# RMSNorm and matmul on one core: weights on the other queue, and PE transposes that carry two bf16 features as one word

## The chip, the cores and the metric

The kernel runs on one core of one Trainium2 chip. The metric is the device time of one execution in microseconds; the figure compared is the median of several runs. The names used: PE is the matmul engine (PEld its weight loads), DVE the vector engine, ACT the scalar engine, POOL the GpSimd engine, and SP the engine that here only issues DMAs. PSUM is the memory that PE writes its results to.

## The reference

`x` is 16 x 1024 rows of 512 features, `weight` is 512 x 768, all float32.

```python
rms = np.sqrt(np.mean(x ** 2, axis=-1, keepdims=True) + eps)
x_norm = x / rms * gamma
return np.matmul(x_norm, weight).astype(np.float32)
```

The kernel computes the same in another order: `gamma` is multiplied into the rows of `weight` once, the matmul runs on raw `x` cast to bf16, and the division by the rms is a scale of the result rows.

## The kernel before

The 16384 rows are cut into 32 groups of 512 (each partition holds 4 consecutive rows), and each group into two pairs: pair `j` is two tiles `t` of 128 rows. The features are cut into K = 4 slices of 128. For a pair, the work passes through the engines like this:

- SP loads a group of `x` (1 MB, line 63), into one of 8 buffers, six groups ahead of its use.
- POOL casts the pair to bf16, `xb` (line 71).
- ACT squares and sums the rows (line 77) and takes the root (line 80); DVE forms the reciprocal, `rstd` (line 82).
- PE transposes the pair's 2 x 4 blocks of 128 x 128 (line 90) into a PSUM tile `tp`, of which there are two; DVE copies `tp` to `xT` (line 92).
- PE multiplies (line 106): for each tile and each k, one matmul of 512 columns and one of 256, with `xT` as the stationary operand and the scaled weights `w_bf` as the moving one, accumulating over k in one of three PSUM buffers `ops`. Each matmul has its own weight load.
- The result is scaled by `rstd` into `ot`: the first tile by ACT (line 110), the second by DVE (line 112). There are four `ot` buffers of one group each.
- SP stores a finished group (1.5 MB, line 116).

Each engine works through its own instructions in the order in which the program writes them. In the loop over pairs this order is: load of group j/2 + 6, cast of pair j+2, squares of j+1, all eight transposes and the copy of j+1, then the matmuls of j, then (every second pair) the store. SP therefore issues the load of a group behind the store of an earlier one, and that store waits until ACT and DVE have written the group.

Ahead of the loop SP queues the first loads of `x`. ACT issues, on its own queue, the load of `gamma` (as 4 rows of 128) and four loads of weight slices. PE transposes `gamma` to `g_sb`, behind the transposes of pair 0, so that partition p holds the factor of feature k x 128 + p. DVE then scales the four weight slices into `w_bf` (line 148) as they come.

Of the kernel before, what the change touches and what calls it, by code (L numbers as in the profile page):

```python
# [12 lines left out]
F32 = mybir.dt.float32  # L13
BF16 = mybir.dt.bfloat16
# [3 lines left out]
@with_exitstack  # L18
def kernel(
    ctx: ExitStack,  # L20
    tc: tile.TileContext,
    x: bass.AP,
    gamma: bass.AP,
    weight: bass.AP,
    eps: float,
    out: bass.AP,
):
    nc = tc.nc
    P = 128

    x = x.flatten_outer_dims()
    out = out.flatten_outer_dims()
    N, D = x.shape
    _, O = out.shape
    K = D // P
    G = 4
    NG = N // (P * G)
    NP = 2 * NG
    PF = 6
    SPLITS = [(0, 512), (512, O)]  # L40


    xg = x.rearrange("(g p t) d -> g p t d", p=P, t=G)
    og = out.rearrange("(g p t) o -> g p t o", p=P, t=G)

    singles = ctx.enter_context(tc.tile_pool(name="singles", bufs=1))
    xin = ctx.enter_context(tc.tile_pool(name="xin", bufs=PF + 2))
    xbp = ctx.enter_context(tc.tile_pool(name="xb", bufs=3))
    junk = ctx.enter_context(tc.tile_pool(name="junk", bufs=2))
    stats = ctx.enter_context(tc.tile_pool(name="stats", bufs=4))  # L50
    xt_pool = ctx.enter_context(tc.tile_pool(name="xt", bufs=3))
    tpsum = ctx.enter_context(tc.tile_pool(name="tpsum", bufs=2, space=bass.MemoryType.PSUM))
    opsum = ctx.enter_context(tc.tile_pool(name="opsum", bufs=3, space=bass.MemoryType.PSUM))
    outp = ctx.enter_context(tc.tile_pool(name="out", bufs=4))

    x_tiles, xb_tiles, rstd_tiles, xT_tiles, o_tiles = {}, {}, {}, {}, {}

    def load(g, parts=1):
        xt = xin.tile([P, G, D], F32, name="xt")
        x_tiles[g] = xt  # L60
        n = G // parts
        for i in range(parts):
            nc.sync.dma_start(out=xt[:, i * n:(i + 1) * n, :], in_=xg[g, :, i * n:(i + 1) * n, :])

    def xpair(j):
        return x_tiles[j // 2][:, 2 * (j % 2):2 * (j % 2) + 2, :]

    def cast(j):
        xb = xbp.tile([P, 2, D], BF16, name="xb")
        xb_tiles[j] = xb  # L70
        nc.gpsimd.tensor_copy(out=xb, in_=xpair(j))  # L71

    def squares(j):
        ssq = stats.tile([P, 2], F32, name="ssq")
        for t in range(2):
            jk = junk.tile([P, D], BF16, name="jk")
            nc.scalar.activation(out=jk, in_=xpair(j)[:, t, :], func=AF.Square,  # L77
                                 accum_out=ssq[:, t:t + 1])
        rms = stats.tile([P, 2], F32, name="rms")
        nc.scalar.activation(out=rms, in_=ssq, func=AF.Sqrt, scale=1.0 / D, bias=eps_sb)  # L80
        rstd = stats.tile([P, 2], F32, name="rstd")
        nc.vector.reciprocal(out=rstd, in_=rms)  # L82
        rstd_tiles[j] = rstd

    def transposes(j):
        xb = xb_tiles.pop(j)
        tp = tpsum.tile([P, 2, K, P], BF16, name="tp")
        for t in range(2):
            for k in range(K):
                nc.tensor.transpose(out=tp[:, t, k, :], in_=xb[:, t, k * P:(k + 1) * P], identity=ident)  # L90
        xT = xt_pool.tile([P, 2, K, P], BF16, name="xT")
        nc.vector.tensor_copy(out=xT, in_=tp)  # L92
        xT_tiles[j] = xT

    def matmuls(j):
        g, h = j // 2, j % 2
        if h == 0:
            o_tiles[g] = outp.tile([P, G, O], F32, name="ot")
        ot = o_tiles[g]
        xT = xT_tiles.pop(j)  # L100
        rstd = rstd_tiles.pop(j)
        for t in range(2):
            ops = opsum.tile([P, 2, 512], F32, name="ops").rearrange("p a b -> p (a b)")
            for k in range(K):
                for lo, hi in SPLITS:
                    nc.tensor.matmul(out=ops[:, lo:hi], lhsT=xT[:, t, k, :], rhs=w_bf[:, k, lo:hi],  # L106
                                     start=(k == 0), stop=(k == K - 1))
            dst = ot[:, 2 * h + t, :]
            if t == 0:
                nc.scalar.mul(out=dst, in_=ops[:, :O], mul=rstd[:, t:t + 1])  # L110
            else:
                nc.vector.tensor_single_scalar(out=dst, in_=ops[:, :O], scalar=rstd[:, t:t + 1],  # L112
                                               op=mybir.AluOpType.mult)

    def store(g, lo=0, hi=G):
        nc.sync.dma_start(out=og[g, :, lo:hi, :], in_=o_tiles[g][:, lo:hi, :])

    with tc.manual_schedule():
        nc.scalar.preload_act_table(AF.Sqrt)  # L119
        load(0, parts=2)  # L120

        g_row = singles.tile([K, P], F32)
        nc.scalar.dma_start(out=g_row, in_=gamma.rearrange("(ko ki) -> ko ki", ki=P))
        w_f32 = singles.tile([P, K, O], F32)
        for k in range(K):
            nc.scalar.dma_start(out=w_f32[:, k, :], in_=weight[k * P:(k + 1) * P, :])  # L126
        for g in range(1, PF):
            load(g)

        ident_f = singles.tile([P, P], F32)  # L130
        make_identity(nc, ident_f)
        ident = singles.tile([P, P], BF16)
        nc.vector.tensor_copy(out=ident, in_=ident_f)  # L133
        eps_sb = singles.tile([P, 1], F32)
        nc.vector.memset(eps_sb, float(eps))

        cast(0)
        cast(1)
        squares(0)
        transposes(0)  # L140

        gp = tpsum.tile([P, K], F32, name="tp")
        nc.tensor.transpose(out=gp, in_=g_row, identity=ident_f[:K, :K])  # L143
        g_sb = singles.tile([P, K], F32)
        nc.vector.tensor_copy(out=g_sb, in_=gp)  # L145
        w_bf = singles.tile([P, K, O], BF16)
        for k in range(K):
            nc.vector.tensor_single_scalar(out=w_bf[:, k, :], in_=w_f32[:, k, :], scalar=g_sb[:, k:k + 1],  # L148
                                           op=mybir.AluOpType.mult)

        for j in range(NP):
            if j % 2 == 0 and j // 2 + PF < NG:
                load(j // 2 + PF)
            if j + 2 < NP:
                cast(j + 2)
            if j + 1 < NP:
                squares(j + 1)
                transposes(j + 1)
            matmuls(j)
            g = j // 2  # L160
            if g == NG - 1:
                store(g, 2 * (j % 2), 2 * (j % 2) + 2)
            elif j % 2:
                store(g)
# [35 lines left out]
```

## Time and profile before

| | us |
|---|---|
| median of 3 runs | 222.38 (222.13 to 222.49) |
| the profiled execution | 222.73 |
| its span, first to last instruction | 221.0 |

| engine | busy us | share of the span |
|---|---|---|
| PE | 198.6 | 90% |
| ACT | 156.1 | 71% |
| DVE | 116.1 | 53% |
| POOL | 67.3 | 30% |

The DMA engines moved 85.73 MB, 388 GB/s over the span. In the page, a row of busy tenths has 40 slices of 5.5 us each, and the GB/s row under it gives what the DMA engines moved in each. A row of a group has the line, the engine, the operation, what it writes and reads, its shape and count, then busy us and mean ns of one, then the idle time of its engine ahead of it and what ended most of that. Matmuls overlap each other, so the mean of one is longer than the distance between two. The chain lists, in order of time, start, duration and the work that set the end. The granted clock of PE was 0.996 on the mean.

### The profile page before, as it was taken

What the parts mean: (1) busy time and instruction counts of PE and PEld (TensorE: products, weight loads), DVE (VectorE), ACT (ScalarE), POOL (GpSimd) and SP (SyncE); (2) the same over time, 40 slices, a digit from 0 to 9 for tenths busy, and PEclk for the clock granted to TensorE, in tenths of its full rate; (3) what the DMA queues carried; (4) which work ended last, traced back from release to release, by engine and by line L of the source; (5) the groups of instructions that cost most, each with busy time, mean ns of one, the idle gap of its engine ahead of it and who ended that gap; (6) DMA issues with size and microseconds to landing.
All of it is one profiled execution on the core that took longest, in us unless ns stands there. A gap on an engine that the chain in (4) does not pass through costs nothing.

```text
span 221.0 us, 4062 instructions
## 1 busy us (share of the span) xinstructions
PE 198.6 (90%) x1508; PEld 130.8 (59%) x1537; DVE 116.1 (53%) x199; ACT 156.1 (71%) x385; POOL 67.3 (30%) x70
## 2 busy tenths in 40 slices
PE   0514999999999999999999999999999999999990
PEld 0302666666666666666666666666666666666660
DVE  0222356655566555665555665556655566555551
ACT  3501577787777887778877778777788777887750
POOL 2440133322333323333233333233332333322000
PEclk9999999999999999999999999999999999999998
DMA  6999379999999999999999999999999999776767
GB/s 199 420 420 425 151 279 395 417 424 423 422 412 428 427 416 429 421 416 420 426 430 426 423 427 429 428 421 426 429 421 425 426 428 415 336 307 291 291 288 285
DMA packets 10108, 85.73 MB, mean 388 GB/s; under 512 B 1124, under 2 KB 1128, under 8 KB 2152
## 3 DMA queue, kind: packets, MB, share of 16 engines
q1 hardware_dynamic: 9504, 83.89, 91.1%
q10 hardware_dynamic: 584, 1.58, 1.8%
q8 instruction: 12, 0.20, 0.3%
q14 instruction: 8, 0.07, 0.1%
HBM read 35.13 MB, written 50.33 MB: 387 GB/s over the span
## 4 chain that ended last, share of the span: by engine, by line
PE 88%; DMA 7%; issue 1%; DVE 1%; ACTq 1%; ACT 0%
PE ops L106 75%; PE tp L90 13%; DMA w_f<-in_weight_dram 7%; ACTq L126 1%; DVE ot L112 0%; DVE w_bf L148 0%; ACT L119 0%
## 5 line engine op out<-in xcount | busy, mean ns | idle before, releaser
L106 PE MATMUL ops<-w_bf,xT 128*128 128x256 bf16 (+1 forms) x995 | 178.4, 328 | 10.3 <-DVE w_bf L148 8.8
L106 PEld LDWEIGHTS <-xT 128*128 128x128 bf16 x1024 | 98.3, 99 | 69.3 <-issue 12.0
L71 POOL CAST xb<-xt 128x1024 bf16<-128x1024 f32 x64 | 66.6, 1042 | 134.6 <-PE tp L90 125.9
L112 DVE TENSOR_SCALAR ot<-ops,rstd 128x768 f32<-128x768 f32 x64 | 65.1, 1018 | 74.3 <-PE ops L106 74.3
L110 ACT ACTIVATE ot<-ops,rstd 128x768 f32<-128x768 f32 x64 | 57.7, 901 | 53.3 <-PE ops L106 53.3
L77 ACT ACTIVATE jk<-xt 128x512 bf16<-128x512 f32 x128 | 78.7, 619 | 3.1 <-DMA xt<-in_x_dram 3.1
L90 PE MATMUL tp<-ident,xb 128*128 128x128 bf16 x512 | 40.3, 223 | 6.8 <-POOL xb L71 6.2
L90 PEld LDWEIGHTS <-xb 128*128 128x128 bf16 x512 | 34.9, 100 | 15.0 <-POOL xb L71 6.7
L92 DVE COPY xT<-tp 128x1024 bf16<-128x1024 bf16 x64 | 43.0, 671 | 0.3 <-PE tp L90 0.3
L77 ACT ACTIVATION_READ_ACCUMULATOR jk<-xt 128x1 f32 x128 | 24.4, 190 | 0.0
L80 ACT ACTIVATE rms<-ssq,eps_sb 128x2 f32<-128x2 f32 x64 | 18.9, 295 | 2.1
L82 DVE RECIPROCAL rstd<-rms 128x2 f32<-128x2 f32 x64 | 10.6, 166 | 15.1 <-ACT rms L80 15.1
L148 DVE TENSOR_SCALAR w_bf<-w_f,g_sb 128x768 bf16<-128x768 f32 x4 | 2.5, 620 | 9.6 <-DMA w_f<-in_weight_dram 9.6
L119 ACT ACT_TABLE_LOAD x1 | 1.3, 1283 | 0.7 <-PEq L181 0.7
L133 DVE CAST ident<-ident_f 128x128 bf16<-128x128 f32 x1 | 0.2, 228 | 1.3 <-POOL ident_f masks.py:199 1.3
masks.py:199 POOL TENSOR_SCALAR_AFFINE_SELECT ident_f<-ident_f 128x128 f32<-128x128 f32 x1 | 0.3, 294 | 0.1
L143 PEld LDWEIGHTS tp<-ident_f,g_row 4*128 4x128 f32 x1 | 0.2, 178 | 0.2 <-issue 0.2
masks.py:197 POOL MEMSET ident_f<- 128x128 f32 x1 | 0.2, 205 | 0.3 <-POOLq L181 0.3
L143 PE MATMUL tp<-ident_f,g_row 4*128 4x4 f32 x1 | 0.3, 264 | 0.0
L181 POOL MEMSET const-float32-0.0<- 128x1 f32 x1 | 0.1, 99 | 0.2 <-issue 0.2
L145 DVE COPY g_sb<-tp 128x4 f32<-128x4 f32 x1 | 0.2, 152 | 0.0
L181 POOL MEMSET const-bfloat16-1.0<- 128x1 bf16 x1 | 0.1, 102 | 0.0
(3 smaller groups left out, 0.3 us busy)
## 6 DMA issues: line engine op xcount, KB each, us to landing
out_dram<-ot SPq DMA_DIRECT2D x31, 1536.0 KB, 9.7
xt<-in_x_dram SPq DMA_DIRECT2D x31, 1024.0 KB, 12.0
w_f<-in_weight_dram ACTq DMA_DIRECT2D x4, 384.0 KB, 12.3
out_dram<-ot SPq DMA_DIRECT2D x2, 768.0 KB, 3.6
xt<-in_x_dram SPq DMA_DIRECT2D x2, 512.0 KB, 4.9
g_row<-in_gamma_dram ACTq DMA_DIRECT2D x1, 2.0 KB
```

The source lines that it names most:

```text
L71: nc.gpsimd.tensor_copy(out=xb, in_=xpair(j))
L77: nc.scalar.activation(out=jk, in_=xpair(j)[:, t, :], func=AF.Square, accum_out=ssq[:, t:t + 1])
L80: nc.scalar.activation(out=rms, in_=ssq, func=AF.Sqrt, scale=1.0 / D, bias=eps_sb)
L82: nc.vector.reciprocal(out=rstd, in_=rms)
L90: nc.tensor.transpose(out=tp[:, t, k, :], in_=xb[:, t, k * P:(k + 1) * P], identity=ident)
L92: nc.vector.tensor_copy(out=xT, in_=tp)
L106: nc.tensor.matmul(out=ops[:, lo:hi], lhsT=xT[:, t, k, :], rhs=w_bf[:, k, lo:hi], start=(k == 0), stop=(k == K - 1))
L110: nc.scalar.mul(out=dst, in_=ops[:, :O], mul=rstd[:, t:t + 1])
L112: nc.vector.tensor_single_scalar(out=dst, in_=ops[:, :O], scalar=rstd[:, t:t + 1], op=mybir.AluOpType.mult)
L119: nc.scalar.preload_act_table(AF.Sqrt)
L126: nc.scalar.dma_start(out=w_f32[:, k, :], in_=weight[k * P:(k + 1) * P, :])
L148: nc.vector.tensor_single_scalar(out=w_bf[:, k, :], in_=w_f32[:, k, :], scalar=g_sb[:, k:k + 1], op=mybir.AluOpType.mult)
```

## The change

**Words instead of halves.** A pair's `xb` is read as 4-byte words, each of which is two neighbouring bf16 features. One PE transpose of a 128 x 128 block of words, with the float32 identity, moves 256 features of 128 rows, so that a pair has four transposes and not eight. Partition w of the result holds, for each row m, the features 2w and 2w + 1 of a half h of 256 features. DVE copies the same number of bf16 elements as before. A matmul for k then reads as its stationary operand `xT[:, t, k // 2, :, k % 2]`, every second element of a row of words. The weights are loaded to fit: partition w holds rows 2w and 2w + 1 of a half, and `gamma` is loaded as 2 x 128 x 2 and transposed in two small steps.

**The order.** Transposes of pair j+2 are written in between the matmuls of pair j, one behind every second 512-column matmul, and the copy to `xT` behind the pair's matmuls. Casts run three pairs ahead; `xb` and `xT` have four buffers and not three. Pair 0 walks k outside and the tile inside, and has the squares of pair 1 and the transposes of pairs 1 and 2 behind it. Gamma's transposes stand first on PE.

**The queues.** The weights come in two DMAs on SP's queue, behind the first half of group 0 and ahead of its second half and of the other groups. Only `gamma` is left on ACT's queue.

```diff
-    xbp = ctx.enter_context(tc.tile_pool(name="xb", bufs=3))
+    xbp = ctx.enter_context(tc.tile_pool(name="xb", bufs=4))
-    xt_pool = ctx.enter_context(tc.tile_pool(name="xt", bufs=3))
+    xt_pool = ctx.enter_context(tc.tile_pool(name="xt", bufs=4))
...
+    def transpose_word(j, t, h):
+        if j not in tp_tiles:
+            tp_tiles[j] = tpsum.tile([P, 2, 2, P], F32, name="tp")
+        words = xb_tiles[j].rearrange("p a d -> p (a d)").bitcast(F32)
+        lo = t * (D // 2) + h * P
+        nc.tensor.transpose(out=tp_tiles[j][:, t, h, :], in_=words[:, lo:lo + P], identity=ident_f)
+
+    def evac_words(j):
+        xb_tiles.pop(j)
+        tp = tp_tiles.pop(j)
+        xT = xt_pool.tile([P, 2, 2, P, 2], BF16, name="xT")
+        nc.vector.tensor_copy(out=xT.rearrange("p t h m c -> p (t h m c)"),
+                              in_=tp.rearrange("p t h m -> p (t h m)").bitcast(BF16))
+        xT_tiles[j] = xT
...
-    def matmuls(j):
+    def matmuls(j, tj=None):
...
+        order = [(t, k) for k in range(K) for t in range(2)] if j == 0 else \
+                [(t, k) for t in range(2) for k in range(K)]
+        for n, (t, k) in enumerate(order):
+            for i, (lo, hi) in enumerate(SPLITS):
+                nc.tensor.matmul(out=acc[t][:, lo:hi], lhsT=xT[:, t, k // 2, :, k % 2], rhs=w_bf[:, k, lo:hi],
+                                 start=(k == 0), stop=(k == K - 1))
+
+                if tj is not None and i == 0 and n % 2 == 0:
+                    transpose_word(tj, n // 4, n // 2 % 2)
...
-        for k in range(K):
-            nc.scalar.dma_start(out=w_f32[:, k, :], in_=weight[k * P:(k + 1) * P, :])
+        nc.sync.dma_start(out=x0[:, 0:2, :], in_=xg[0, :, 0:2, :])
+        for h in range(2):
+            nc.sync.dma_start(out=w_f32[:, 2 * h:2 * h + 2, :],
+                              in_=weight[2 * h * P:2 * (h + 1) * P, :].rearrange("(w c) o -> w c o", c=2))
+        nc.sync.dma_start(out=x0[:, 2:4, :], in_=xg[0, :, 2:4, :])
...
-            if j + 2 < NP:
-                cast(j + 2)
-            if j + 1 < NP:
-                squares(j + 1)
-                transposes(j + 1)
-            matmuls(j)
+            if j + 3 < NP:
+                cast(j + 3)
+            if j == 0:
+                cast(2)
+                matmuls(0)
+                squares(1)
+                transposes(1)
+                transposes(2)
+            else:
+                if j + 1 < NP:
+                    squares(j + 1)
+                if j + 2 < NP:
+                    matmuls(j, j + 2)
+                    evac_words(j + 2)
+                else:
+                    matmuls(j)
```

How the instructions stand, at three places. In PE's program inside the loop, before, the last of the eight transposes of a pair and the first matmuls behind it (the numbers tell buffers apart; "waits" names the engines whose work the instruction needs):

```order
L90 LDWEIGHTS xb_149
L90 MATMUL tp_203<-ident_110,xb_149 128x128
L106 LDWEIGHTS xT_169 [waits DVE_49]
L106 MATMUL ops_214<-w_bf_142,xT_169 128x512
L106 LDWEIGHTS xT_169
L106 MATMUL ops_214<-w_bf_142,xT_169 128x256
```

and of the change, the start of pair 1's matmuls with the first transpose of pair 3 among them:

```order
L121 LDWEIGHTS xT_181 [waits DVE_49]
L121 MATMUL ops_201<-w_bf_135,xT_181 128x512
L92 MATMUL tp_204<-ident_f_103,xb_142 128x128 [waits PE_49]
L121 LDWEIGHTS xT_181
L121 MATMUL ops_201<-w_bf_135,xT_181 128x256
```

The transpose has moved between the 512- and the 256-column matmul, and its weight load is part of the float32 instruction and not a row of its own.

In SP's program at the start, before (`xt` is a group's buffer, `ot` the result's; DMAHW is an earlier DMA whose slot is used again):

```order
L63 DMA xt<-in_x_dram 128x1024 x2
L63 DMA xt<-in_x_dram 128x2048
L63 DMA xt<-in_x_dram 128x2048 [waits DMAHW0_49]
L63 DMA xt<-in_x_dram 128x2048 [waits DMAHW1_49]
L63 DMA xt<-in_x_dram 128x2048 [waits DMAHW2_49]
L63 DMA xt<-in_x_dram 128x2048 [waits DMAHW3_49]
L63 DMA xt<-in_x_dram 128x2048 [waits DMAHW4_49]
L116 DMA out_dram<-ot 128x3072 [waits DMAHW5_49,DVE_49,Activation_49]
L63 DMA xt<-in_x_dram 128x2048 [waits DMAHW6_49]
```

and of the change:

```order
L146 DMA xt<-in_x_dram 128x1024
L148 DMA w_f_87<-in_weight_dram 128x1536 x2
L150 DMA xt<-in_x_dram 128x1024
L63 DMA xt<-in_x_dram 128x2048 x3
L63 DMA xt<-in_x_dram 128x2048 [waits DMAHW0_49]
L63 DMA xt<-in_x_dram 128x2048 [waits DMAHW1_49]
L63 DMA xt<-in_x_dram 128x2048 [waits DMAHW2_49]
L136 DMA out_dram<-ot 128x3072 [waits DMAHW3_49,DVE_49,Activation_49]
L63 DMA xt<-in_x_dram 128x2048 [waits DMAHW4_49]
```

The two weight DMAs have come into this list, ahead of all of `x` but half a group; the first store stands behind the same seven groups as before.

In DVE's program at the start, before, from the scaling of the weights on:

```order
L148 TENSOR_SCALAR w_bf<-w_f_90,g_sb 128x768 [waits DMAHW3_49,DVE_49]
L148 TENSOR_SCALAR w_bf<-w_f_90,g_sb 128x768 [waits DMAHW4_49]
L148 TENSOR_SCALAR w_bf<-w_f_90,g_sb 128x768 [waits DMAHW6_49]
L148 TENSOR_SCALAR w_bf<-w_f_90,g_sb 128x768 [waits DMAHW7_49]
L82 RECIPROCAL rstd<-rms 128x2 [waits Activation_49]
L92 COPY xT<-tp 128x1024 [waits PE_49]
L112 TENSOR_SCALAR ot<-ops,rstd 128x768 [waits PE_49]
```

and of the change:

```order
L172 TENSOR_SCALAR w_bf<-w_f_87,g_sb 128x768 [waits DMAHW2_49,DVE_49]
L172 TENSOR_SCALAR w_bf<-w_f_87,g_sb 128x768
L172 TENSOR_SCALAR w_bf<-w_f_87,g_sb 128x768 [waits DMAHW3_49]
L172 TENSOR_SCALAR w_bf<-w_f_87,g_sb 128x768
L132 TENSOR_SCALAR ot<-ops,rstd 128x768 [waits DVE_49,PE_49]
L82 RECIPROCAL rstd<-rms 128x2 [waits Activation_49]
L98 COPY xT<-tp 128x1024 [waits PE_49] x2
```

The copy of pair 1 and its reciprocal, which stood ahead of pair 0's evacuation, now stand behind it.

More of the change, by code (lines that the diff above doesn't have):

```diff
@@ L83, in squares @@
         rstd_tiles[j] = rstd
+    def transpose_word(j, t, h):
[11 more added lines that the diff above has]
+        xT_tiles[j] = xT
     def transposes(j):
-        xb = xb_tiles.pop(j)
-        tp = tpsum.tile([P, 2, K, P], BF16, name="tp")
         for t in range(2):
-            for k in range(K):
[L90 to L93, printed above, removed]
-    def matmuls(j):
+            for h in range(2):
+                transpose_word(j, t, h)
+        evac_words(j)
+    def matmuls(j, tj=None):
         g, h = j // 2, j % 2
@@ L101, in matmuls @@
         rstd = rstd_tiles.pop(j)
[L102 to L107, printed above, removed]
+        acc = [opsum.tile([P, 2, 512], F32, name="ops").rearrange("p a b -> p (a b)") for _ in range(2)]
+        order = [(t, k) for k in range(K) for t in range(2)] if j == 0 else \
[6 more added lines that the diff above has]
+                    transpose_word(tj, n // 4, n // 2 % 2)
+            if k < K - 1:
+                continue
             dst = ot[:, 2 * h + t, :]
             if t == 0:
-                nc.scalar.mul(out=dst, in_=ops[:, :O], mul=rstd[:, t:t + 1])
+                nc.scalar.mul(out=dst, in_=acc[t][:, :O], mul=rstd[:, t:t + 1])
             else:
-                nc.vector.tensor_single_scalar(out=dst, in_=ops[:, :O], scalar=rstd[:, t:t + 1],
+                nc.vector.tensor_single_scalar(out=dst, in_=acc[t][:, :O], scalar=rstd[:, t:t + 1],
                                                op=mybir.AluOpType.mult)
@@ L119 @@
         nc.scalar.preload_act_table(AF.Sqrt)
-        load(0, parts=2)
-        g_row = singles.tile([K, P], F32)
-        nc.scalar.dma_start(out=g_row, in_=gamma.rearrange("(ko ki) -> ko ki", ki=P))
+        g_row = singles.tile([2, P, 2], F32)
+        nc.scalar.dma_start(out=g_row, in_=gamma.rearrange("(h w c) -> h w c", w=P, c=2))
         w_f32 = singles.tile([P, K, O], F32)
-        for k in range(K):
-            nc.scalar.dma_start(out=w_f32[:, k, :], in_=weight[k * P:(k + 1) * P, :])
+        x0 = xin.tile([P, G, D], F32, name="xt")
+        x_tiles[0] = x0
+        nc.sync.dma_start(out=x0[:, 0:2, :], in_=xg[0, :, 0:2, :])
+        for h in range(2):
+            nc.sync.dma_start(out=w_f32[:, 2 * h:2 * h + 2, :],
+                              in_=weight[2 * h * P:2 * (h + 1) * P, :].rearrange("(w c) o -> w c o", c=2))
+        nc.sync.dma_start(out=x0[:, 2:4, :], in_=xg[0, :, 2:4, :])
         for g in range(1, PF):
@@ L131 @@
         make_identity(nc, ident_f)
-        ident = singles.tile([P, P], BF16)
-        nc.vector.tensor_copy(out=ident, in_=ident_f)
         eps_sb = singles.tile([P, 1], F32)
         nc.vector.memset(eps_sb, float(eps))
+        gp = tpsum.tile([P, 2, 2], F32, name="tp")
+        for c in range(2):
+            nc.tensor.transpose(out=gp[:, c, :], in_=g_row[:, :, c], identity=ident_f[:2, :2])
+        g_sb = singles.tile([P, 2, 2], F32)
+        nc.vector.tensor_copy(out=g_sb, in_=gp)
         cast(0)
@@ L140 @@
         transposes(0)
[L142 to L145, printed above, removed]
         w_bf = singles.tile([P, K, O], BF16)
         for k in range(K):
-            nc.vector.tensor_single_scalar(out=w_bf[:, k, :], in_=w_f32[:, k, :], scalar=g_sb[:, k:k + 1],
+            nc.vector.tensor_single_scalar(out=w_bf[:, k, :], in_=w_f32[:, k, :], scalar=g_sb[:, k % 2, k // 2:k // 2 + 1],
                                            op=mybir.AluOpType.mult)
```

2 lines of the change are left out of this document (1 added, 1 removed).

## The prediction

> **What bounds the kernel now.** I read the page first: busy shares, slices, chain.
>
> ```profile
> PE 198.6 (90%) x1508; PEld 130.8 (59%) x1537; DVE 116.1 (53%) x199; ACT 156.1 (71%) x385; POOL 67.3 (30%) x70
> PE   0514999999999999999999999999999999999990
> DMA  6999379999999999999999999999999999776767
> GB/s 199 420 420 425 151 279 395 417 424 423 422 412 428 427 416 429 421 416 420 426 430 426 423 427 429 428 421 426 429 421 425 426 428 415 336 307 291 291 288 285
> DMA packets 10108, 85.73 MB, mean 388 GB/s; under 512 B 1124, under 2 KB 1128, under 8 KB 2152
> PE 88%; DMA 7%; issue 1%; DVE 1%; ACTq 1%; ACT 0%
> ```
>
> PE carries the chain, but look at the DMA row: from slice 8 to slice 33 the engines are full as well. Two limits lie almost on each other, with a hole in DMA near slice 5 and slack at the end. The chain in order of time gives the PE side:
>
> ```profile
> 2.98 16.52 DMA w_f<-in_weight_dram
> 19.53 0.63 DVE w_bf L148
> 20.20 3.35 PE ops L106 x10
> ...
> 27.66 2.60 PE ops L106 x16
> 30.26 0.45 PE tp L90 x8
> ...
> 211.16 4.51 PE ops L106 x27
> 215.70 1.02 DVE ot L112
> ```
>
> The loop cannot start until the last weight slice has come, at 19.5. After that a pair costs 2.60 + 0.45 = 3.05 us, without gaps (64 x 3.05 = 195.2; 20.2 to 215.7 is 195.5). The first ten matmuls after the wait take 335 ns each, the later ones 2.60/16 = 163: a start-up price of PE after idling. The DMA side, by stretches (columns: length, busy us of PE, PEld, DVE, ACT, POOL, then granted clock, DMA share, GB/s):
>
> ```profile
> 5.00:10.00 5.00, 2.35 (x18) 2.00 (x19) 1.55 (x4) 3.24 (x10) 2.08 (x2) 1.00 1.02 418
> 20.00:25.00 5.00, 4.80 (x22) 2.66 (x22) 2.21 (x6) 2.41 (x6) 0.46 (x1) 1.00 0.82 344
> 25.00:30.00 5.00, 4.95 (x37) 3.19 (x37) 2.04 (x4) 3.42 (x8) 1.63 (x2) 1.00 0.19 79
> 40.00:60.00 20.00, 19.84 (x154) 13.14 (x155) 11.84 (x21) 15.58 (x40) 7.26 (x7) 1.00 1.01 422
> 100.00:120.00 20.00, 19.84 (x159) 13.30 (x160) 11.82 (x21) 15.98 (x41) 7.07 (x7) 1.00 1.01 427
> 195.00:200.00 5.00, 4.95 (x39) 3.20 (x38) 3.36 (x6) 3.74 (x11) 2.08 (x2) 1.00 0.63 263
> 200.00:205.00 5.00, 4.95 (x42) 3.39 (x42) 2.79 (x4) 4.34 (x12) 1.04 (x1) 1.00 0.68 285
> 210.00:215.00 5.00, 4.95 (x37) 3.13 (x36) 2.79 (x4) 2.67 (x7) 0.00 (x0) 1.00 0.67 279
> ```
>
> A full DMA moves 418 GB/s while only loads run, 422 to 427 with loads and stores mixed, and, from 263/0.63, 285/0.68 and 279/0.67, about 417 with stores alone. At 20 to 30 it runs dry: the first seven groups have landed, the first store is not there yet, and the next load stands behind that store in SP's program. That costs 0.9 + 4.05 = 5 us of DMA. After 190, with nothing left to load, it idles a third.
>
> **The change part by part.** (1) *Transposes.* Per pair eight bf16 transposes go and four 4-byte ones come. What one costs, p, is the first unknown:
>
> ```profile
> L106 PEld LDWEIGHTS <-xT 128*128 128x128 bf16 x1024 | 98.3, 99 | 69.3 <-issue 12.0
> L90 PE MATMUL tp<-ident,xb 128*128 128x128 bf16 x512 | 40.3, 223 | 6.8 <-POOL xb L71 6.2 <-DVE xT L92 0.6
> L90 PEld LDWEIGHTS <-xb 128*128 128x128 bf16 x512 | 34.9, 100 | 15.0 <-POOL xb L71 6.7 <-issue 0.3
> L143 PE MATMUL tp<-ident_f,g_row 4*128 4x4 f32 x1 | 0.3, 264 | 0.0
> L143 PEld LDWEIGHTS tp<-ident_f,g_row 4*128 4x128 f32 x1 | 0.2, 178 | 0.2 <-issue 0.2
> ```
>
> A bf16 transpose has a pitch of 0.45/8 = 56 ns, though its weight load alone shows 100: loads hide behind the matmul before. The one f32 transpose (gamma) is one load and one matmul, so I count one pass, not several; its load takes 178 ns instead of 100. In the new order each 4-byte load stands behind a 512-column matmul, which by columns has 2/3 of two pitches, 217 ns: 178 fits. The matmul streams 128 columns: 56 ns if a 4-byte column goes at the speed of a 2-byte one, 112 if at half. The low bound of p is 56 (a gain below that has no row), the high one 178 + 56 = 234 (load not hidden). I take 56 to 90: one pass is what the row shows, and there are as many columns as before.
>
> (2) *The 1024 matmuls* keep their count, each with its load as before, but the stationary operand is read with a step of two elements. If that load grew from 99 to 178 it would still hide behind 217, but not behind a transpose of 56 or quite behind a 256-column matmul of 108; bounds 0 and 79 ns at four places a pair, which act like p + 79. I take 0.
>
> (3) *Spreading, four buffers.* Transposes of j+2 run inside the matmuls of j. Evacuation keeps its 1024 bf16 elements and its price, and now has a pair's time until its use. If that cover went, PE would wait out one copy a pair, 0.67 us.
>
> (4) *Weights on SP's queue.* They stand behind half of group 0 alone. From the start:
>
> ```profile
> 5.12 1.04 POOL L71 CAST xb<-xt 128x1024 bf16<-128x1024 f32 x1 [3.82 <-DMA xt<-in_x_dram]
> 7.29 0.69 DVE L92 COPY xT<-tp 128x1024 bf16<-128x1024 bf16 x1 [0.34 <-PE tp L90]
> 9.22 0.62 DVE L148 TENSOR_SCALAR w_bf<-w_f,g_sb 128x768 bf16<-128x768 f32 x1 [1.17 <-DMA w_f<-in_weight_dram]
> 21.03 0.90 ACT L110 ACTIVATE ot<-ops,rstd 128x768 f32<-128x768 f32 x1 [12.64 <-PE ops L106]
> 21.83 0.62 ACT L77 ACTIVATE jk<-xt 128x512 bf16<-128x512 f32 x1
> 23.19 0.29 ACT L80 ACTIVATE rms<-ssq,eps_sb 128x2 f32<-128x2 f32 x1
> 24.53 0.16 DVE L82 RECIPROCAL rstd<-rms 128x2 f32<-128x2 f32 x1
> 24.60 0.67 DVE L92 COPY xT<-tp 128x1024 bf16<-128x1024 bf16 x1
> 28.35 0.35 SPq L116 DMA_DIRECT2D out_dram<-ot  x1
> ```
>
> Slice 0 moved 199 x 5.525 = 1.10 MB, 2.6 us at 420, so the stream starts at 2.9. The first 0.52 MB landed at 5.1, so landing trails moving by 0.95. Weight halves of 0.79 MB then land at 2.9 + 1.31/0.42 + 0.95 = 7.0 and at 8.9. DVE finishes xT(0) near 7.7 and scales four slices at 0.62 each: 8.3 to 10.2. Pair 0 walks k outside, starts at 8.4, and takes 3.35 + 6 x 0.163 = 4.3 us: 12.7. Then comes a new wait. On DVE xT(1) stands behind rstd(1), and that behind ACT: evacuation 0.90, squares and root 21.83 to 23.48 = 1.65, rstd 0.17, copy 0.67. From 12.5 this gives pair 1 a start at **15.9**; PE idles 2 us there. (Group 1 lands near 12.5 and its two casts end at 14.6, so the transposes of pair 2 fit in.) The remaining pairs, two of them without transposes: PE ends at 15.9 + 61 x (2.60 + 4p) + 2 x 2.60 = 179.7 + 244p (p in us). Add 5.3 from PE's end to the span's (215.7 to 221.0) and 222.38 - 221.0 = 1.4 to the median of the runs (the profiled run itself took 222.73). The **PE path** is thus 186.4 + 244p: 200.0 at 56 ns.
>
> (5) *DMA* moves the same 85.73 MB. The first store can be issued about 15.9 + 2.8 + 1.0 = 19.7 (28.35 now), and the first 8.9 MB (seven groups and weights) last until 2.9 + 8.9/0.42 = 24.1: the hole closes with 4.4 us to spare. A pair moves 1.31 MB: at 2.82 us PE would ask for 465 GB/s. So stores pile up until the four output buffers, then ACT and DVE, hold PE back, and what piled up fills the slack at the end. **DMA path**: 7.1 MB at 418 to 420 (17.0 us), 66.1 MB at 424 (155.9), 12.5 MB at 417 (30.0): 202.9. Add 2.9 before, and after it 1.9: the last 0.77 MB store had 4.2 us from issue at 216.8 to 221.0, of which 1.9 is moving and some of the rest hides in a full queue.
>
> ```profile
> 205.04 12.07 SPq L116 DMA_DIRECT2D out_dram<-ot  x4
> ```
>
> Span 207.7, profiled run 1.7 more, against the median of 222.38: **209.0 us**. With 427 throughout it is 206.6, with 420 and the whole 2.3 behind it 210.7: its own range.
>
> The rates above are rows. [...]
>
> **The rivals.** *A 4-byte column at half speed.* p near 112, or a slower strided load that acts like it. PE path 213.7, pairs of 3.05 as now and only the start won. For: four words carry the bytes of eight halves. Against: one pass in the gamma row. From p = 93 on PE sets the end instead of DMA.
>
> *The 4-byte weight load is not hidden* (slower). Its place is PE between the 512- and the 256-column matmul: if the load must wait for the running matmul to leave the array, each transpose stands 178 + 56 = 234 ns in the path, a pair takes 3.54, and the result is **243.5**. It decides from p = 148 on, where 186.4 + 244p meets 222.4. For: gamma's load is the only one of its kind and stood alone. Against: 1536 bf16 loads of 99 ns all hid. [...]
>
> *The start does not move as planned.* If gamma's little load, now first on PE, or pair 1's chain came over 4.4 us later, the DMA hole would return, at worst with all its 5 us: 214.
>
> **How the numbers follow.** DMA-bound 0.62 at 209.0; half speed 0.20, between 209 and 222; load not hidden 0.13; start late 0.05. The range takes the first case's low end and most of the second: 206.6 to 216. A measurement of this kernel tells 0.2% from no change. Faster 0.85 (0.62 + 0.05 + 0.18), same 0.02, slower 0.13.
>
> **What would show it.** DMA share near 1.0 from 5 us to within a few us of the end, no dip at 20 to 30, and no 0.65 after 190. PE below 90% busy, with waits on output buffers, that is ACT and DVE waiting on stores. Pair 1 starting near 16 behind xT. Matmul stretches of about 2.82 us a pair where PE runs freely. If pairs take 3.0 without waits and DMA is under 0.95, it is half speed; if 3.2 or more, with PE idle at loads, it is the unhidden load. A weight wait beyond 10 us proves (4) wrong.

## The result and the profile after

| | before | changed |
|---|---|---|
| median of 4 runs, us | 222.44 (222.13 to 222.61) | 214.58 (214.20 to 215.21) |
| the profiled execution, us | 222.73 | 214.2 |
| its span, us | 221.0 | 212.4 |

The ratio is 0.9651, with a 95% interval of 0.9624 to 0.9678: 3.5% faster. The forecast was 209.0 with a range of 206.6 to 216.0. The sign and the range hold, and the likeliest case does not: what came is the first rival, a word that passes at half speed (109 ns a transpose, against 56 for one of bf16), which the prediction priced at 213.7 and gave a chance of 0.20.

The page of the changed kernel, with the rows that answer to those of before:

```profile
PE 197.4 (93%) x1282; PEld 136.8 (64%) x1282; DVE 110.7 (52%) x198; ACT 156.4 (74%) x385; POOL 67.3 (32%) x70
PE   0569999999999999999999999999999999999990
DMA  6999999999999999999999999999999999977777
GB/s 180 420 427 423 417 427 429 423 422 420 430 430 422 427 427 423 428 426 430 421 428 423 427 425 433 425 426 433 415 425 428 430 427 427 413 296 303 305 301 292
PE 92%; DMA 2%; DVE 1%; ACT 1%; POOL 0%; issue 0%
L92 PE MATMUL tp<-ident_f,xb 128*128 128x128 f32 x256 | 68.9, 275 | 5.5 <-POOL xb L71 5.5
L92 PEld LDWEIGHTS tp<-ident_f,xb 128*128 128x128 f32 x256 | 36.0, 142 | 8.7 <-POOL xb L71 5.9
```

The hole in the DMA row near slice 5 is gone. The slack at the end is not, and PE carries the chain without a gap, as before. Stretches of the changed kernel (columns as in the prediction):

```profile
160.00:180.00 20.00, 20.00 (x134) 13.97 (x133) 10.74 (x20) 15.86 (x39) 6.41 (x7) 1.00 1.01 426
195.00:200.00 5.00, 5.00 (x35) 3.49 (x33) 3.28 (x6) 3.77 (x12) 0.00 (x0) 1.00 0.59 248
```

From 16.0 to 206.6 PE is never idle (190.60 us busy of 190.60). DMA is full up to about 180 and 0.59 busy at 195: the engine that sets the end is PE. Its timeline shows why. First the end of pair 0 and the start of pair 1, with eight transposes between them, then a stretch of the loop:

```profile
12.83 0.60 PE L92 MATMUL tp<-ident_f,xb 128*128 128x128 f32 x4
15.13 0.66 PE L92 MATMUL tp<-ident_f,xb 128*128 128x128 f32 x4 [1.70 <-POOL xb L71]
16.00 0.39 PE L121 MATMUL ops<-w_bf,xT 128*128 128x512 bf16 x1 [0.21 <-DVE xT L98]
```

```profile
100.49 0.27 PE L92 MATMUL tp<-ident_f,xb 128*128 128x128 f32 x1
100.60 0.81 PE L121 MATMUL ops<-w_bf,xT 128*128 128x256 bf16 x4
101.25 0.27 PE L92 MATMUL tp<-ident_f,xb 128*128 128x128 f32 x1
```

The matmul behind a word transpose starts 0.11 us after it (100.49 to 100.60), where a bf16 one took 0.056. From one transpose to the next are 0.76 us, of which four matmuls are 0.65. Over the loop it is 0.759 (16.22 to 100.49 in 111 steps), so p = 0.109, and a pair takes 4 x 0.759 = 3.04 us against 3.05 before. Four words of 109 ns cost what eight halves of 56 cost. PE's end moved from 215.7 to 206.65, that is 9.05 us: pair 1 starts 8.2 us earlier (24.2 to 16.0), the 0.01 us a pair bring some 0.6, and the rest is that before, PE was not yet at full speed in pair 1 (its matmuls span 3.00 us from 24.21, those of pair 2 only 2.76).

### The profile page after: what moved, and what is told of

It reads as the page before. It is cut to its first block, busy times and chain, and to the rows that moved or that the text cites. A ratio compares the mean times of both kernels' runs of the same rounds, so it can differ in the third digit from the quotient of the medians.

```text
span 212.4 us, 3581 instructions
## 1 busy us (share of the span) xinstructions
PE 197.4 (93%) x1282; PEld 136.8 (64%) x1282; DVE 110.7 (52%) x198; ACT 156.4 (74%) x385; POOL 67.3 (32%) x70
## 4 chain that ended last, share of the span: by engine, by line
PE 92%; DMA 2%; DVE 1%; ACT 1%; POOL 0%; issue 0%
PE ops L121 79%; PE tp L92 13%; DMA xt<-in_x_dram 2%; ACT jk L77 1%; POOL xb L71 0%; DVE ot L132 0%; ACT ot L130 0%; DVE xT L98 0%; DVE w_bf L172 0%; ACT rms L80 0%; DVE rstd L82 0%
## 5 line engine op out<-in xcount | busy, mean ns | idle before, releaser
L121 PE MATMUL ops<-w_bf,xT 128*128 128x512 bf16 (+1 forms) x1024 | 194.8, 327 | 1.5 <-DVE w_bf L172 1.3
L121 PEld LDWEIGHTS <-xT 128*128 128x128 bf16 x1024 | 100.6, 98 | 58.5 <-issue 1.8
L92 PE MATMUL tp<-ident_f,xb 128*128 128x128 f32 x256 | 68.9, 275 | 5.5 <-POOL xb L71 5.5
L98 DVE COPY xT<-tp 128x1024 bf16<-128x1024 bf16 x64 | 43.5, 681 | 0.4 <-PE tp L92 0.4
L92 PEld LDWEIGHTS tp<-ident_f,xb 128*128 128x128 f32 x256 | 36.0, 142 | 8.7 <-POOL xb L71 5.9
L82 DVE RECIPROCAL rstd<-rms 128x2 f32<-128x2 f32 x64 | 10.0, 156 | 5.6 <-ACT rms L80 5.6
```

What stands on the lines that cost most here:

```text
L92: nc.tensor.transpose(out=tp_tiles[j][:, t, h, :], in_=words[:, lo:lo + P], identity=ident_f)
L98: nc.vector.tensor_copy(out=xT.rearrange("p t h m c -> p (t h m c)"), in_=tp.rearrange("p t h m -> p (t h m)").bitcast(BF16))
L121: nc.tensor.matmul(out=acc[t][:, lo:hi], lhsT=xT[:, t, k // 2, :, k % 2], rhs=w_bf[:, k, lo:hi], start=(k == 0), stop=(k == K - 1))
```

## The experiments

Two theories went into the first four runs. **S**: the array takes a 4-byte column at half the speed of a 2-byte one, 128 x 2 columns at the matmuls' own rate. **L**: a weight load sets the 109 ns, either the word load or the strided bf16 load behind it, which 56 ns cannot hide. A fourth run measures the DMA path by itself. The other four split the change and try to beat it. Ratios are to the kernel before, run on the same chip.

### Half the columns, the same loads

```diff
-        nc.tensor.transpose(out=tp_tiles[j][:, t, h, :], in_=words[:, lo:lo + P], identity=ident_f)
+        for r in (0, P // 2):
+            nc.tensor.transpose(out=tp_tiles[j][:, t, h, r:r + P // 2], in_=words[0:P // 2, lo:lo + P],
+                                identity=ident_f[0:P // 2, 0:P // 2])
```

> Each word transpose becomes two that load 128 columns of words but stream only 64 columns each (rows 0 to 63 of a tile go into both halves; rows 64 to 127 are left out). Theory S, a 4-byte column streams at half the speed of a 2-byte one: two times 64 columns cost what 128 did, about 112 ns for both in place of 109, pairs of 3.05 us, 214 to 216 us in all. Rival L, what sets the 109 ns is a weight load that cannot hide (the one behind the transpose, with a step of two elements, or the word load itself): two loads in a row cost 200 ns or more, pairs of 3.4 us or more, about 236 us.

Measured: 281.85 us, a single run, against 222.68, and neither theory's number. The loop in this kernel: PE, then the word loads (one load's shortest, middle and longest duration in ns; the sum and count of their waits; and a place in the timeline):

```profile
100.27 0.33 PE L93 MATMUL tp<-ident_f,xb 64*128 64x64 f32 x2
100.54 0.82 PE L123 MATMUL ops<-w_bf,xT 128*128 128x256 bf16 x4
```

```profile
L93 PEld LDWEIGHTS tp<-ident_f,xb x40: 135/138/141, 100.3 to 119.8; 64*128 64x128 f32 x40
PEld tp L93 <- issue: 78.7, 245, 0.6
101.29 0.20 PEld L93 LDWEIGHTS tp<-ident_f,xb 64*128 64x128 f32 x2 [0.32 <-issue]
```

The edit brought a cost of its own: operands of 64 rows. Their load no longer runs ahead under the matmul in front, as the 128-row word load of the changed kernel does (142 ns from 100.28, its transpose at 100.49), but stands idle for 0.32 us and starts with its own transpose; that wait sums to 78.7 us. So the total says nothing on S and L. The inside of a place does: two loads of 128 columns take 0.20 us and one of them 0.138, so the second starts 0.06 us behind the first. Word loads can follow each other at 60 ns when 64 columns stream between them; in the changed kernel, with 128 columns, four in a row stand 0.109 apart ((0.60 - 0.273)/3 from the row at 12.83). One load is as long as there (138 against 142 ns), so the load does not set the distance, and this speaks for S. The edit halves the rows with the columns, though, so that it does not tell these two apart.

### Weight loads with unit step

```diff
-        xT = xt_pool.tile([P, 2, 2, P, 2], BF16, name="xT")
-        nc.vector.tensor_copy(out=xT.rearrange("p t h m c -> p (t h m c)"), ...
+        xT = xt_pool.tile([P, 2, 2, 2, P], BF16, name="xT")
+        nc.vector.tensor_copy(out=xT.rearrange("p t h c m -> p (t h) m c"), ...
...
-    ... lhsT=xT[:, t, k // 2, :, k % 2], ...
+    ... lhsT=xT[:, t, k // 2, k % 2, :], ...
```

> DVE's copy sorts the two features of each word apart, so that the matmuls' weight loads read with unit step as in the kernel before; the word transposes stay. S: nothing changes on PE, 0.759 us from transpose to transpose, pairs of 3.036, 214.2 to 215.2 us, if DVE stays under 3 us a pair (its copy may take 1.1 us in place of 0.68). L, by the strided load: the transpose falls to 56 ns, pairs to 2.83, and the time to the DMA path, 209 to 211 us.

Measured: 369.48 us, ratio 1.658 (1.654 to 1.662). The condition in the expectation was far off (its 1.1 us for the copy was the author's guess; no run shows it): DVE's copy, which now writes the two halves of a word 128 elements apart, takes 4.7 us in place of 0.68, and DVE became the bound.

```profile
L98 DVE COPY xT<-tp 128x1024 bf16<-128x1024 bf16 x64 | 300.6, 4703 | 0.4 <-PE tp L92 0.4
100.70 0.39 PE L121 MATMUL ops<-w_bf,xT 128*128 128x512 bf16 x1 [2.19 <-DVE rstd L82]
100.93 0.27 PE L92 MATMUL tp<-ident_f,xb 128*128 128x128 f32 x1
101.04 0.93 PE L121 MATMUL ops<-w_bf,xT 128*128 128x256 bf16 x4
101.76 0.42 PE L92 MATMUL tp<-ident_f,xb 128*128 128x128 f32 x1
101.97 1.49 PE L121 MATMUL ops<-w_bf,xT 128*128 128x256 bf16 x4
```

PE now waits for DVE's `rstd` 61 times (2.19 us ahead of the matmuls at 100.70), and in places it runs at half speed: the granted clock is 0.87 over the run, and at 101.97 four matmuls take 1.49 us in place of 0.81. The place ahead of that can be read, since its transpose takes 0.27 us as in the changed kernel, and not 0.42 as the one at 101.76: with a unit-step load behind it, the next matmul again starts 0.11 us after the transpose (100.93 to 101.04), as S says. With a strided load, a unit-step load and another word load behind it, the transpose costs 0.11 each time. L by the strided load falls.

### Old transposes, spread

Two bf16 transposes at each of the four places, with the plain layout of weights and gamma; the rest as in the changed kernel.

```diff
-            tp_tiles[j] = tpsum.tile([P, 2, 2, P], F32, name="tp")
...
-        nc.tensor.transpose(out=tp_tiles[j][:, t, h, :], in_=words[:, lo:lo + P], identity=ident_f)
+            tp_tiles[j] = tpsum.tile([P, 2, K, P], BF16, name="tp")
+        for k in (2 * h, 2 * h + 1):
+            nc.tensor.transpose(out=tp_tiles[j][:, t, k, :], in_=xb_tiles[j][:, t, k * P:(k + 1) * P], identity=ident)
...
```

> The changed kernel with the old transposes: eight of bf16 a pair, two at each of the four places, plain layout of weights and gamma; early weights, order and buffers stay. S: two bf16 transposes at 56 ns cost 112 where a word one cost 109: pairs of 3.05 and 215 to 216 us, so that the words bring under 1 us of the gain of 7.9. L: the unit-step loads hide, pairs of 3.05 as well. If spreading itself has a price, a place costs more than 112 ns.

Measured: 215.56 us, ratio 0.9671 (0.9645 to 0.9698), as expected. The interval overlaps that of the changed kernel. PE at its start and in its loop:

```profile
8.81 5.28 PE L119 MATMUL ops<-w_bf,xT 128*128 128x512 bf16 x16 [1.31 <-DVE w_bf L171]
16.78 0.39 PE L119 MATMUL ops<-w_bf,xT 128*128 128x512 bf16 x1 [0.75 <-DVE xT L97]
17.01 0.28 PE L91 MATMUL tp<-ident,xb 128*128 128x128 bf16 x2
...
23.86 0.28 PE L91 MATMUL tp<-ident,xb 128*128 128x128 bf16 x2
```

From 17.01 to 23.86 are nine places at 0.761 us, against 0.759 with words: over 244 places some 0.5 us. Pair 1 starts 0.8 us later, since pair 0 ran slowly throughout here (5.28 us; 4.17 in the changed kernel); whether the old transposes or chance made it slow, no run shows. In the loop the words are worth about 0.5 us of the 7.9, and spreading has no price on PE.

### No transposes in the loop

```diff
-        xT = xT_tiles.pop(j)
+        xT = xT_tiles[min(j, 2)]
...
-                if j + 2 < NP:
-                    matmuls(j, j + 2)
-                    evac_words(j + 2)
-                else:
-                    matmuls(j)
+                matmuls(j)
```

> From pair 3 on the transposes and their copies are left out and the matmuls read pair 2's xT, so the output is wrong from there; loads, casts, squares and stores stay. PE needs 2.60 us a pair. My DMA path: the DMA engines are full from 5 us to the end, 209.0 us (206.6 to 210.7). Rival, the DMA engines could move more than 424 GB/s if PE asked for it: the PE path with pairs of 2.60, 16 + 63 x 2.60 + 5 + 2 = 187 us. Rival, contention makes full DMA slower: above 211 us.

Measured: 211.68 us, ratio 0.9499 (0.9477 to 0.9521): above the range given for the DMA path, and 25 us above what PE alone would need. So DMA does become the bound when PE is faster, and its path is 2.7 us longer than predicted. The waits (their sum in us, their number, the longest) show the mechanism that the prediction described, and the stretches show the end, where the time was lost:

```profile
PE ops L121 <- ACT ot L130: 15.8, 17, 1.5
ACT ot L130 <- DMA out_dram<-ot: 15.1, 11, 2.1
DVE ot L132 <- DMA out_dram<-ot: 9.1, 7, 1.9
```

```profile
160.00:180.00 20.00, 17.15 (x105) 9.99 (x103) 6.86 (x12) 14.16 (x36) 6.07 (x6) 1.00 1.02 430
200.00:204.00 4.00, 0.00 (x0) 0.00 (x0) 0.41 (x1) 0.00 (x0) 0.00 (x0) 0.83 0.97 404
204.00:205.00 1.00, 0.00 (x0) 0.00 (x0) 0.00 (x0) 0.00 (x0) 0.00 (x0) 0.50 0.40 166
207.00:208.00 1.00, 0.00 (x0) 0.00 (x0) 0.00 (x0) 0.00 (x0) 0.00 (x0) 0.50 0.06 25
```

ACT and DVE wait for stores to free the output buffers, PE waits for ACT, and the rate is what was forecast or better, up to 430 GB/s. But from 204 us on it falls: 166 GB/s, then 55, then 25 until 208, where the DMA engines are 0.06 busy. That is the rate of one of sixteen (430/16 = 27): the engines do not finish together. Whether it was one and the same engine is not shown. The 283 KB moved after 204 would have been through at 204.7 at full rate, 1.1 us earlier than predicted (205.8); the span ended 5.2 us behind that and not 1.9, and the median lies 1.8 above the span and not 1.3. Together these are the 2.7 us.

### The weights alone

The kernel before, with old transposes, order and buffers, and only the two weight DMAs put on SP's queue.

```diff
-        load(0, parts=2)
...
-        for k in range(K):
-            nc.scalar.dma_start(out=w_f32[:, k, :], in_=weight[k * P:(k + 1) * P, :])
+        nc.sync.dma_start(out=x0[:, 0:2, :], in_=xg[0, :, 0:2, :])
+        for h in range(2):
+            nc.sync.dma_start(out=w_f32[:, 2 * h:2 * h + 2, :], ...)
+        nc.sync.dma_start(out=x0[:, 2:4, :], in_=xg[0, :, 2:4, :])
```

> The kernel before with only the two weight DMAs moved to SP's queue, behind the first half of group 0; old transposes, order and buffers. Theory, the gain is the start: the transposes of pair 1 stand ahead of pair 0's matmuls and wait for the cast of the second half of group 0 (about 11.5), pair 0 starts near 12.4 and pair 1's matmuls near 17.2 (24.2 before, 16.0 in the changed kernel); 215.5 to 216.5 us. Rival, the gain is the transposes' or their spreading: 220 us or more.

Measured: 215.92 us against 222.87, ratio 0.9688 (0.9665 to 0.9710), as expected.

```profile
12.30 1.03 PE L90 MATMUL tp<-ident,xb 128*128 128x128 bf16 x8 [4.58 <-POOL xb L71]
13.13 3.93 PE L106 MATMUL ops<-w_bf,xT 128*128 128x512 bf16 x16
16.89 0.61 PE L90 MATMUL tp<-ident,xb 128*128 128x128 bf16 x8
17.34 2.76 PE L106 MATMUL ops<-w_bf,xT 128*128 128x512 bf16 x15
```

Pair 1's matmuls start at 17.34 (17.2 expected). This one edit brings 3.1 of the 3.5%. The 0.4% left for words, order and buffers together is not clear of noise, since the two intervals overlap; in the traces PE ends 1.9 us later here (208.59 against 206.65), of which the start makes 1.3. The edit changes the queue, the place ahead of `x` and the number of DMAs at once, and no run tells these apart.

### Everything but the weights

```diff
-        for h in range(2):
-            nc.sync.dma_start(out=w_f32[:, 2 * h:2 * h + 2, :], ...)
+        for k in range(K):
+            nc.scalar.dma_start(out=w_f32[:, k, :],
+                                in_=weight.rearrange("(h w c) o -> h c w o", w=P, c=2)[k // 2, k % 2])
```

> The changed kernel with the weights as before, four slices on ACT's queue; words, order and buffers stay. Theory: the last slice lands near 19.5 again, pair 1 starts near 24.6, pairs of 3.03 us; 221.0 to 222.5 us, so the words and the new order alone bring 1 us or less. Rival: 216 to 218 us.

Measured: 224.08 us, ratio 1.0056 (1.0035 to 1.0077): 0.6% slower than before, and a miss by 1.6 us. Pair 1 starts at 23.91, ahead of the 24.6 expected, but PE is slow there:

```profile
19.77 1.44 PE L121 MATMUL ops<-w_bf,xT 128*128 128x512 bf16 x4 [2.02 <-DVE w_bf L172]
23.91 0.61 PE L121 MATMUL ops<-w_bf,xT 128*128 128x512 bf16 x1 [0.99 <-DVE xT L98]
...
27.51 1.49 PE L121 MATMUL ops<-w_bf,xT 128*128 128x256 bf16 x4
...
29.83 0.81 PE L121 MATMUL ops<-w_bf,xT 128*128 128x256 bf16 x4
```

The same four matmuls are over in 1.49 us at 27.5 and in 0.81 at 29.8. With k outside, pair 0 is four short bursts behind four late slices, and PE starts pair 1 at half speed. In the kernel before, half of pair 0 (the second tile) was left when the last slice came; those ran through behind the first tile's last two (ten matmuls, 3.35 us from 20.20), and PE was nearly at speed by 24 (pair 1 started at 24.21 and lost 0.2 us). That the short bursts are why PE stayed slow is read from the two timelines; no run changes them alone. The granted clock does not tell them apart: it reads 1.00 from 20 to 30 us before, and 0.9 or more in every slice of that stretch here. Full speed came near 29, some 5 us after pair 1's start. So by this reading pair 0's new order costs time when the weights come late; whether it beats the old one when they come early, no run tests by itself.

### A shorter chain into pair 1

```diff
-                matmuls(0)
-                squares(1)
-                transposes(1)
-                transposes(2)
+                matmuls(0, at={4: [(1, 0, 0)], 5: [(1, 0, 1), (1, 1, 0)], 6: [(1, 1, 1)]}, mid=(6, 1))
+                squares(1)
+            elif j == 1:
...
+                matmuls(1, at={3: [(2, 0, 0)], 4: [(2, 0, 1)], 5: [(2, 1, 0), (2, 1, 1)],
+                               6: [(3, 0, 0), (3, 0, 1)], 7: [(3, 1, 0), (3, 1, 1)]}, mid=(5, 2))
+                evac_words(3)
```

(`at` gives the word transposes behind step n of the matmuls, `mid` the step behind which DVE's copy of a pair is issued.)

> The changed kernel with pair 1's chain cut: the transposes of pair 1 stand among pair 0's matmuls, its copy to xT ahead of pair 0's evacuation and of its own reciprocal, and the transposes of pairs 2 and 3 among pair 1's matmuls. Theory, PE sets the end: pair 1 starts near 13.1 in place of 16.0, and the time falls by the same, to 211.7, where the DMA path (211.7 in the run without transposes) is reached: 211.5 to 213. Rival, the start no longer matters because DMA already sets the end: 214 to 215.

Measured: 213.75 us, ratio 0.9592 (0.9572 to 0.9613): faster than the changed kernel, and less than expected; it lies between the two ranges given.

```profile
14.48 1.37 PE L121 MATMUL ops<-w_bf,xT 128*128 128x512 bf16 x7 [0.35 <-DVE xT L98]
...
18.70 0.39 PE L121 MATMUL ops<-w_bf,xT 128*128 128x512 bf16 x1 [0.56 <-DVE xT L98]
```

Pair 1 starts 1.5 us earlier, but pair 2 only 0.3 (18.70 against 16.00 + 3.04 = 19.04), and PE's end follows pair 2: 206.31 against 206.65. The trace thus accounts for 0.3 of the 0.8 us between the medians; the rest stays open (the changed kernel's own runs lie 1.0 apart). The eight transposes that filled part of the gap now stand inside pairs 0 and 1, and pair 2 waits 0.56 us for its copy. I had counted the whole gap as idle; of the 3.2 us from 12.83 to 16.00 PE had spent 1.3 on transposes.

### The start at full speed

The short chain, with the second half of group 0 queued between the weight halves, and identity matmuls that keep PE busy until the weights are there. Pair 1's four transposes all stand behind step 3 of pair 0 here.

```diff
+        for _ in range(WARM):    # 34
+            nc.tensor.matmul(out=warm[:, :P], lhsT=ident, rhs=ident, start=True, stop=True)
         transposes(0)
+        for _ in range(WARM2):   # 12
+            nc.tensor.matmul(out=warm[:, :P], lhsT=ident, rhs=ident, start=True, stop=True)
...
+            if h == 0:
+                nc.sync.dma_start(out=x0[:, 2:4, :], in_=xg[0, :, 2:4, :])
-        nc.sync.dma_start(out=x0[:, 2:4, :], in_=xg[0, :, 2:4, :])
```

> The kernel with the cut chain, the second half of group 0 queued between the two weight halves, and 46 small bf16 matmuls of the identity, written to an unused PSUM buffer, while PE waits for the weights, so that pair 0 runs at 163 ns a matmul and not at 335. PE alone: pair 1 starts near 12.2, one more us saved. Theory, two limits: with PE no longer alone in setting the end, 211 to 212.5, hardly below the cut chain. Rival, PE still sets it alone: a full us below the cut chain.

Measured: 212.40 us, ratio 0.9529 (0.9513 to 0.9546). It beats both kernels.

```profile
2.51 3.81 PE L179 MATMUL ops<-ident 128*128 128x128 bf16 x34
8.57 1.35 PE L122 MATMUL ops<-w_bf,xT 128*128 128x512 bf16 x6 [0.64 <-DVE w_bf L186]
...
17.16 0.39 PE L122 MATMUL ops<-w_bf,xT 128*128 128x512 bf16 x1 [0.59 <-DVE xT L99]
204.77 1.02 DVE L138 TENSOR_SCALAR ot<-ops,rstd 128x768 f32<-128x768 f32 x1 [1.58 <-PE ops L122]
```

Pair 0's first seven matmuls (six of them in the trace) take 1.35 us, as seven at full speed do in the run without transposes (at 104.87). Pair 2 starts at 17.16, which is 1.9 us ahead of the changed kernel, and the last evacuation (204.77 against 206.65) keeps all of it. The time falls 1.35 us below the short chain: the rival's number, PE alone still sets the end. The 212.40 also lies within the range given for the theory of two limits, but by luck: that theory had the start bring hardly anything, and the trace shows all of it kept. The 211.7 of the run without transposes lies just below and was not reached.

## Why the prediction was right, and where it was not

**The step that failed** is part (1), "I take 56 to 90". The argument was that the gamma row shows one load and one matmul, and that there are as many columns as before. The count was right and the conclusion was not: the row tells how many passes there are and nothing about the speed of one, and gamma's four columns are too few to show it. Measured, p = 109 ns, close to "112 if at half". The distance was 60 ns with 64 columns and 109 with 128, and it did not depend on the load that comes behind, which is what S says. Plain half speed, 256 columns at the matmuls' rate, gives 2.60/16 x 256/384 = 108.

**What followed from it.** With p = 109 the prediction's own sum 186.4 + 244p gives 213.0, and DMA no longer sets the end, as said for p over 93. The measured 214.58 is 1.6 more: PE ended 0.3 us later than its sum, from PE's end to the span's took 5.75 us and not 5.3, and the median of the runs lies 2.2 above the span and not 1.4 (this term took the median of several runs and the span of one; the profiled runs themselves lie 1.7 and 1.8 above their spans). The result is inside the range because the range took in most of this rival, not because the likeliest case was right.

**The start**, part (4), came as worked out, term by term:

```profile
8.16 2.20 DVE L172 TENSOR_SCALAR w_bf<-w_f,g_sb 128x768 bf16<-128x768 f32 x4
8.82 4.17 PE L121 MATMUL ops<-w_bf,xT 128*128 128x512 bf16 x16 [1.31 <-DVE w_bf L172]
12.70 0.90 ACT L130 ACTIVATE ot<-ops,rstd 128x768 f32<-128x768 f32 x1 [5.76 <-PE ops L121]
15.19 0.17 DVE L82 RECIPROCAL rstd<-rms 128x2 f32<-128x2 f32 x1 [1.14 <-ACT rms L80]
15.27 1.27 DVE L98 COPY xT<-tp 128x1024 bf16<-128x1024 bf16 x2
20.34 0.35 SPq L136 DMA_DIRECT2D out_dram<-ot  x1
```

The scaling ends at 10.4 (10.2), pair 0 starts at 8.8 (8.4), pair 1 at 16.0 (15.9) behind the chain that was named, and the first store goes out at 20.3 (19.7), in time to close the hole in DMA. The margin was thin at one place: pair 2's transposes waited for POOL until 15.13 and were over 0.2 us before pair 1. The run with the weights alone shows that this part is nearly the whole gain.

**The strided loads**, part (2), cost nothing, as taken: 98 ns each, as before, and four matmuls in 0.65 us. **Spreading and buffers**, part (3), brought nothing that PE shows. **The unhidden load**, the slower rival, fell: the 142 ns of the word load lie under the 512-column matmul, and no place of the loop shows PE waiting for it. Gamma's 178 ns, on which the term rested, had been read while PE was slow; a bf16 load at 8.73 in the trace of before took 147 and not 98.

**The DMA path**, part (5), was not reached by the change. Where it was reached, without transposes, it measured 211.7 and not 209.0 (own range up to 210.7): the rate was right, and the term of 1.9 us behind the moving was too small, since the DMA engines ended unevenly there (5.2 us). Why they did stays open.

**Chances.** The forecast of faster held for the reason that it shared with the rival, the start; 0.62 on the DMA-bound case was too much for a p that no row of before had measured.

## What to carry to other kernels

Count what an operation streams and at what speed, not how many instructions there are: here packing two elements into one word halved the transposes and left the time on PE, with 109 ns for a word transpose against 56. This kernel, whose loop is full, won by an earlier start (3.1 of the 3.5%), so look at when the first operand that the whole loop needs comes, and at what is loaded ahead of it, before the loop is touched. An order written for early data (k outside) can be worse than the old one where the data come late, as read here from the timelines of a run 0.6% slower than before, so a change of several parts should be taken apart both ways.

## What the runs showed of the hardware beyond that

- A 128 x 128 transpose of 4-byte words costs 109 ns of PE at full speed, whichever load is behind it, against 56 for 2-byte elements.
- DVE's copy of 1024 bf16 elements out of PSUM takes 0.68 us in order and 4.7 us when neighbouring elements are written 128 elements apart.
- Word transposes on 64 rows between matmuls on 128 rows lost the cover of their weight load: 0.32 us of waiting at each place.
- In the one run whose DMA was full to the end, the last transfers did not end together: the rate fell to 166, 55 and then 25 GB/s, a sixteenth, over 4 us. In the changed kernel it fell from 326 GB/s to nothing within 1 us.
- In the run where DVE was the bound and PE waited for its `rstd` 61 times (2.7 us at most), PE lost its speed for stretches: granted clock 0.87 over the run, and four matmuls in 1.49 us at 101.97 in place of 0.81. That the waits are the cause is not tested.
